# Two heads' value products in turns: a change to groups B and D of a two-layer hybrid decoder on Trainium2

## The chip, the cores and the metric

The kernel runs on one core of a Trainium2 chip, in one launch. The metric is the device time of an execution in microseconds (us), the median of several runs. Profiles are of one execution taken by the hardware profiler; times in them are counted from the first instruction.

Engines in the profile: PE is the matrix engine, PEld its weight loads, DVE is VectorE, ACT is ScalarE, POOL is GpSimd, SP issues most of the DMAs. Matrix products are written to PSUM, which has 8 banks. TensorE's two clock levels are 1.2 and 2.4 GHz; the profile shows the granted clock as a share of full speed.

## What is computed

One sequence of 1024 tokens with 1024 channels passes through two layers. Each layer has a token mixing part with four groups of 256 channels (4 heads of 64 each) and then a mixture of experts. The groups are: A (RWKV-7, a recurrence), B (stick-breaking attention), C (mLSTM, chunks) and D (attention over the 256 best keys of an indexer, one key and value head for all query heads). Cut to groups B and D:

```python
def stick_breaking_attn(q, k, v):                 # group B
    for i in range(S // 128):                     # blocks of 128 queries
        z = q[block i] . k[: 128 * (i + 1)] * scale
        ...
        outs.append(einsum('bhqk,bkhd->bqhd', att, v[:, :kl]))

def dsa_attn(q, k, v, qi, ki, wi):                # group D
    for i in range(S // 128):
        ...
        prob = softmax(logits of the chosen keys)
        outs.append(einsum('bhqn,bqnd->bhqd', prob, vs))   # one v for all heads
```

The value product of a block, a head and 128 keys is the piece of the last line of each: 64 value channels by 128 queries, summed over the key blocks 0 to i.

## The kernel before

A layer's mixing part is written as Python generators that a planner, weave (L196), takes in turns by a virtual time: each step of a stream adds the matrix work that it issued, or 0.2 where it issued none, both over the stream's pace. The program order that comes out is the order of priority; a scheduler then places each instruction in the queue of its engine when its inputs are expected, and each engine executes its queue in order. After the projections, four streams run side by side: group A (pace 260); group D, then C, then B (paces 350 and 140, one after the other in one stream); the modulation vectors (the ada weights); and the output projection, which waits for finished pieces of the groups.

Groups B and D run over two column tiles ct of two heads each, two groups f of four blocks, and the blocks i of 128 queries. For each block two generators, one per head, are stepped in turns. In B (Stick.unit, L561) a head's steps are: scores into PSUM tag "a", a copy to z, Exp and Ln into e; then a mask on POOL, a reversed running sum on DVE (L580), a subtraction (L582), Exp; then transposes of z on PE (L148), a copy of them into at, which is e's memory, and the value products. B has three pairs of z and e, handed round as (2i + h) mod 3. In D (Dsa.unit, L1112) a head has two steps, with z ("dz") and at ("dat") from a shared pool of 23 large tiles.

The products of a head stand at the end of its last step. The output tile py has 128 partitions: head 0 of the pair fills partitions 0 to 63 and head 1 partitions 64 to 127, which are the two halves of PE's columns. py comes from PSUM tag "b", which has three banks that group A and others share. It is taken by whichever head comes first, and copied out when both heads are done. All products go through the helper k.mm, so their line in the profile is L143; in the profile B's products are b<-e,sv and D's are b<-dat,dv. They are fp32, 128 rows by 64 columns with 128 elements of moving data, and the profile shows each as two records. In group A, b<-tl, pj<-tl,ra and pj<-ra,tl are an inverse by doubling, ya the output. Group C has one product of the same kind as the value products, b<-v,kw (L793), whose loop over heads alternates the halves.

Copies out of PSUM by k.ev go to DVE and ACT in turns, by one counter for all streams.

Of the kernel before, what the change touches and what calls it, by code (L numbers as in the profile page):

```python
# [244 lines left out]
class Rwkv:  # L245
# [261 lines left out]
    def run(self, width=3):  # L507
        self.job = {}
        jobs = [(ct, hf) for hf in range(2) for ct in range(2)]
        yield from self.prep(*jobs[0])  # L510
        units = [(ct, 0, nb) for ct in range(2) for nb in range(4)] + [(ct, 1, nb) for nb in range(4) for ct in range(2)]
        ahead = {(0, 0, 1): jobs[1], (1, 0, 0): jobs[2], (1, 0, 2): jobs[3]}
        live, side = [], []
        k = self.k
        free = [(k.med("ra"), k.med("bkv", 384), k.med("mp"), k.big("tl", 1024)) for _ in range(width)]
        while units or live or side:
            while units and len(live) < width and units[0][:2] in self.job and "bon" in self.job[units[0][:2]]:
                u = units.pop(0)
                own = free.pop(0)
                live.append((u, self.unit(*u, own), own))  # L520
                if u in ahead:
                    side.append(self.prep(*ahead[u]))
            for it in list(live):
                try:
                    next(it[1])
                    yield
                except StopIteration:
                    live.remove(it)
                    free.append(it[2])
                    if it[0][2] % 2:  # L530
                        side.append(self.out(*it[0][:2], it[0][2] // 2))
            for g in list(side):
                try:
                    next(g)
                    yield
                except StopIteration:
                    side.remove(g)
# [13 lines left out]
    V.scalar_tensor_tensor(y, y, g, sq, op0=ALU.mult, op1=ALU.mult)  # L551


class Stick:


# [1 line left out]
        self.k, self.pc = k, pc  # L558
        self.qk, self.y, self.done = {}, {}, set()

    def unit(self, i, h, py, own):  # L561
        k, nc = self.k, self.k.nc
        V, G = nc.vector, nc.gpsimd
        hs = slice(64 * (h % 2), 64 * (h % 2) + 64)
        q, kt = self.qk[i // 4, h // 2]
        q = q[:, 512 * (h % 2) + 128 * (i % 4):512 * (h % 2) + 128 * (i % 4) + 128]
        kl = 128 * (i + 1)
        z, e = own
        for o in range(0, kl, 512):
            n = min(512, kl - o)  # L570
            pz = k.psum("a", n)
            k.mm(pz, q, kt[h % 2][0][:, o:o + n], stop=False)
            k.mm(pz, q, kt[h % 2][1][:, o:o + n], start=False)
            V.tensor_scalar(z[:, o:o + n], pz, 40.0, None, op0=ALU.min)
        k.act(e[:, :kl], z[:, :kl], AF.Exp)
        k.act(e[:, :kl], e[:, :kl], AF.Ln, bias=1.0)
        yield
        dg = slice(kl - 128, kl)
        G.tensor_tensor(e[:, dg], e[:, dg], k.c("sl"), op=ALU.mult)
        V.tensor_tensor_scan(e[:, :kl][:, ::-1], e[:, :kl][:, ::-1], e[:, :kl][:, ::-1], initial=0.0,  # L580
                             op0=ALU.add, op1=ALU.bypass)
        V.tensor_tensor(z[:, :kl], z[:, :kl], e[:, :kl], op=ALU.subtract)  # L582
        k.act(z[:, :kl], z[:, :kl], AF.Exp)
        G.tensor_tensor(z[:, dg], z[:, dg], k.c("sl"), op=ALU.mult)
        yield
        at = e
        for o in range(0, kl, 512):
            n = min(512, kl - o)
            pt = k.psum("a", n)
            for b in range(n // 128):  # L590
                k.tr(pt[:, 128 * b:128 * b + 128], z[:, o + 128 * b:o + 128 * b + 128])
            k.ev(at[:, o:o + n], pt)
        if not py:
            py.append(k.psum("b", 128))
        for b in range(i + 1):
            k.mm(py[0][hs], self.v[:, b, hs], at[:, 128 * b:128 * b + 128],
                 start=b == 0, stop=b == i)
        yield

    def run(self, tk, l):  # L600
        k = self.k
        groups = [(f, ct) for f in range(2) for ct in range(2)]
        own = [(k.big("z"), k.big("e")) for _ in range(3)]
        self.load(tk, l, *groups[0])
        for g, (f, ct) in enumerate(groups):
            if g > 1:
                self.load(tk, l, f, ct)
            n = 4 * f + 4
            self.v = k.big("sv", 128 * n).rearrange("p (n c) -> p n c", n=n)
            k.nc.sync.dma_start(self.v, tk.pk[l][0:128 * n, 128 * ct:128 * ct + 128].rearrange("(n p) c -> p n c", p=P))  # L610
            y = k.med("yb")
            self.y[ct, f] = y
            for i in range(4 * f, 4 * f + 4):
                if i == 2 and g == 0:
                    self.load(tk, l, *groups[1])
                py = []
                gens = [self.unit(i, 2 * ct + h, py, own[(2 * i + h) % 3]) for h in range(2)]
                while gens:
                    for n in list(gens):
                        try:  # L620
                            next(n)
                            yield
                        except StopIteration:
                            gens.remove(n)
                k.ev(y[:, 128 * (i % 4):128 * (i % 4) + 128], py[0])
            head_norm(k, y, self.pc("sbg", ct), eps=self.eps)
            self.done.add((ct, f))
            yield
# [233 lines left out]
class Dsa:  # L862
# [246 lines left out]
            V.tensor_scalar(key[i], key[i], 1.0, -NEG, op0=ALU.subtract, op1=ALU.mult)  # L1109
            yield 4.0  # L1110

    def unit(self, i, h, py):  # L1112
        k, nc = self.k, self.k.nc
        V = nc.vector
        kl = 128 * (i + 1)
        hs = slice(64 * (h % 2), 64 * (h % 2) + 64)
        o = 512 * (h % 2) + 128 * (i % 4)
        q = self.q[i // 4, h // 2][:, o:o + 128]
        neg = self.neg[i] if i >= 2 else self.zd[:, 256 - kl:256]
        z = k.big("dz")  # L1120
        mx = k.small("dmx", 2, bufs=4)
        for o in range(0, kl, 512):
            n = min(512, kl - o)
            p = k.psum("a", n)
            k.mm(p, q, self.kh[:, o:o + n], stop=False)
            k.mm(p, q, self.kl[:, o:o + n], start=False)
            V.tensor_tensor_reduce(z[:, o:o + n], p, neg[:, o:o + n], 1.0, 2 * NEG if o == 0 else mx[:, 0:1],
                                   op0=ALU.add, op1=ALU.max, accum_out=mx[:, 0:1] if o == 0 else mx[:, 1:2])
        last = mx[:, 0:1] if kl <= 512 else mx[:, 1:2]
        nb = k.small("dnb", 1, bufs=4)  # L1130
        V.tensor_scalar(nb, last, -0.125, None, op0=ALU.mult)
        k.act(z[:, :kl], z[:, :kl], AF.Exp, scale=0.125, bias=nb, accum_out=self.ssum[:, 4 * i + h:4 * i + h + 1])
        yield
        at = k.big("dat")
        for o in range(0, kl, 512):
            n = min(512, kl - o)
            pt = k.psum("pj", n)
            for b in range(n // 128):
                k.tr(pt[:, 128 * b:128 * b + 128], z[:, o + 128 * b:o + 128 * b + 128])
            k.ev(at[:, o:o + n], pt)  # L1140
        if not py:
            py.append(k.psum("b", 128))
        for b in range(i + 1):
            k.mm(py[0][hs], self.v[:, b, :], at[:, 128 * b:128 * b + 128], start=b == 0, stop=b == i)
        yield

    def load(self, f, ct):
# [6 lines left out]
    def run(self):  # L1154
        k = self.k
        self.y, self.q = {}, {}
        groups = [(f, ct) for f in range(2) for ct in range(2)]
        self.load(*groups[0])
        for g, (f, ct) in enumerate(groups):
            y = k.med("yd")  # L1160
            self.y[ct, f] = y
            for i in range(4 * f, 4 * f + 4):
                if i % 4 == 2 and g < 3:
                    self.load(*groups[g + 1])
                py = []
                gens = [self.unit(i, 2 * ct + h, py) for h in range(2)]
                while gens:
                    for n in list(gens):
                        try:
                            next(n)  # L1170
                            yield
                        except StopIteration:
                            gens.remove(n)
                k.ev(y[:, 128 * (i % 4):128 * (i % 4) + 128], py[0])
            if ct:
                yield from self.finish(f)

# [1024 lines left out]
```

## Time and profile before

| | |
|---|---|
| median of 3 runs | 3668.0 us (3665.5 to 3668.82) |
| profiled execution, timed | 3678.16 us |
| its span in the profile | 3676.4 us |
| granted TensorE clock, mean | 0.922 |
| busy PE / DVE / ACT / POOL | 88% / 76% / 53% / 23% |
| mixing part of layer 0, groups D, C, B | 430 to 1215 us |
| mixing part of layer 1, groups D, C, B | 2280 to 3030 us |
| experts | 1215 to 1900 us and 3030 us to the end |

The page gives one line of busy time per engine, 40 slices, the DMA queues, the chain of work that ended last, and the costliest groups of instructions. A matrix instruction's start is recorded and its end is modelled, so records overlap and a busy PE is not PE at its peak. What one stretch is limited by is read from views that are cut to that stretch.

### The profile page before, as it was taken

How to read it: one execution, taken by the hardware profiler on the slowest of the kernel's cores; microseconds unless marked ns; L12 is line 12 of the kernel's file. 1: busy time of each engine (PE TensorE's matmuls, PEld its weight loads, DVE VectorE, ACT ScalarE, POOL GpSimd, SP SyncE). 2: the span in 40 equal slices, each digit the busy share in tenths (PEclk: the TensorE clock that was granted, in tenths of full speed). 3: DMA queues.
4: the chain of work that ended last, by engine and by line, in shares of the span. 5: the costliest groups of instructions: out<-in, count | busy, mean ns of one | idle time of the engine just before them, and what ended most of it. 6: DMA issues, size and time to landing. Idle time of an engine off the chain costs nothing.

```text
span 3676.4 us, 54588 instructions
## 1 busy us (share of the span) xinstructions
PE 3234.4 (88%) x18848; PEld 2542.0 (69%) x18848; DVE 2779.7 (76%) x5552; ACT 1935.2 (53%) x3324; POOL 841.2 (23%) x769
## 2 busy tenths in 40 slices
PE   6888889998888799999958888999898879999996
PEld 3876645576667678777757766767676667877775
DVE  4589843457766799999965998555777679999995
ACT  3456332234444577777753662432444447777774
POOL 3220110113322113322312202111223221342221
PEclk8989999998998899999979888989998879999998
DMA  5222355433433899999931233023344369999996
GB/s 195 76 87 91 118 189 195 168 125 98 135 115 140 277 363 385 379 385 383 357 116 53 92 93 102 17 70 111 112 128 118 118 241 364 381 380 387 383 381 216
DMA packets 373671, 746.61 MB, mean 203 GB/s; under 512 B 44235, under 2 KB 108385, under 8 KB 373393
## 3 DMA queue, kind: packets, MB, share of 16 engines
q1 hardware_dynamic: 346880, 672.03, 51.0%
q0 software_dynamic: 20256, 70.33, 7.3%
q8 instruction: 150, 2.46, 0.3%
q10 hardware_dynamic: 6256, 0.74, 0.1%
q14 instruction: 129, 1.05, 0.1%
HBM read 635.45 MB, written 107.53 MB: 202 GB/s over the span
## 4 chain that ended last, share of the span: by engine, by line
PE 49%; DVE 21%; DMA 18%; issue 5%; ACT 4%; POOL 1%; SPq 1%; ACTq 0%; DVEq 0%; POOLq 0%
PE pj L143 25%; PE b L143 16%; DMA wr<-in_moe_w_dram 12%; DVE dkey L1017 5%; PE a L143 3%; PE a L148 3%; DVE e L580 1%; PE pj L148 1%; DMA out_dram<-yo,si 1%; DVE wl L1530 1%; DMA xs<-yo,si 1%; PE b L148 1%; DVE z L582 1%; ACT wh L160 1%; DVE h L1780 1%
## 5 line engine op out<-in xcount | busy, mean ns | idle before, releaser
L160 ACT ACTIVATE wh<-wr 128x1024 fp32r<-128x1024 f32 (+3 forms) x900 | 888.6, 1005 | 296.6 <-DMA wr<-in_moe_w_dram 133.1
L1530 DVE TENSOR_TENSOR wl<-wr,wh 128x1024 fp32r<-128x1024 f32 x792 | 938.3, 1220 | 59.7 <-ACT wh L160 47.7
L143 PE MATMUL pj<-wl,xh 128*128 128x512 f32 x1056 | 419.3, 403 | 15.9 <-DVE wl L1530 15.4
L143 PE MATMUL pj<-wh,xh 128*128 128x512 f32 x1056 | 421.2, 400 | 11.3 <-ACT xh L160 11.2
L143 PE MATMUL pj<-wh,xl 128*128 128x512 f32 x1056 | 419.7, 397 | 0.0
L143 PEld LDWEIGHTS pj<-wl,xh 128*128 128x128 f32 x1056 | 200.0, 190 | 83.6 <-DVE wl L1530 39.4
L143 PEld LDWEIGHTS pj<-wh,xh 128*128 128x128 f32 x1056 | 200.1, 190 | 55.5 <-ACT xh L160 13.8
L143 PEld LDWEIGHTS pj<-wh,xl 128*128 128x128 f32 x1056 | 200.6, 190 | 45.8 <-DVE xl L1542 0.8
L143 PE MATMUL b<-wh,hh 128*128 128x512 f32 x528 | 210.5, 399 | 12.3 <-ACT wh L160 11.3
L1426 POOL DMA_INDIRECT xg<-h2d,si x64 | 74.7, 1167 | 630.9 <-PE a L148 375.7
L143 PE MATMUL pj<-hh,wh 128*128 128x512 f32 x480 | 197.4, 412 | 14.6 <-ACT wh L160 5.7
L143 PE MATMUL b<-wh,hl 128*128 128x512 f32 x528 | 208.2, 394 | 0.7 <-DVE hl L1542 0.7
L143 PE MATMUL pj<-hh,wl 128*128 128x512 f32 x480 | 196.3, 409 | 6.4 <-DVE wl L1855 6.4
L143 PE MATMUL pj<-wh,hh 128*128 128x256 f32 (+2 forms) x640 | 187.6, 306 | 16.1 <-DVE stl L1972 11.6
L143 PE MATMUL pj<-wh,hl 128*128 128x256 f32 (+2 forms) x640 | 192.4, 302 | 3.3 <-DVE hl L1832 3.3
L143 PE MATMUL pj<-hl,wh 128*128 128x512 f32 x480 | 194.4, 405 | 0.0
L143 PE MATMUL pj<-wl,hh 128*128 128x256 f32 (+2 forms) x640 | 188.9, 297 | 2.8 <-POOL wl L1855 2.8
L160 ACT ACTIVATE ra<-b 128x256 f32<-128x256 f32 x192 | 73.2, 383 | 222.5 <-PE b L143 220.2
L143 PE MATMUL b<-wl,hh 128*128 128x512 f32 x528 | 175.1, 410 | 2.2 <-DVE wl L1530 2.1
L1497 POOL DMA_INDIRECT out_dram<-yo,si x32 | 141.4, 4419 | 137.4 <-DVE yo L1494 122.7
L1497 POOL DMA_INDIRECT xs<-yo,si x32 | 136.3, 4260 | 133.5 <-DVE yo L1494 119.4
L421 DVE TENSOR_TENSOR tl<-pj,tl 128x512 f32<-128x512 f32 x128 | 87.1, 686 | 99.0 <-PE pj L143 98.0
(524 smaller groups left out, 7819.6 us busy)
## 6 DMA issues: line engine op xcount, KB each, us to landing
wr<-in_moe_w_dram SPq DMA_DIRECT2D x792, 512.0 KB
aw<-in_ada_w_dram SPq DMA_DIRECT2D x96, 512.0 KB
wr<-in_w_in_dram SPq DMA_DIRECT2D x84, 256.0 KB
wo<-in_w_out_dram SPq DMA_DIRECT2D x48, 256.0 KB
xs<-xp SPq DMA_DIRECT2D x48, 256.0 KB
xp<-xs SPq DMA_DIRECT2D x48, 256.0 KB
out_dram<-xp SPq DMA_DIRECT2D x48, 256.0 KB
sk<-pt SPq DMA_DIRECT2D x32, 256.0 KB
```

The source lines that it names most:

```text
L143: return self.nc.tensor.matmul(out, lhsT, rhs, start=start, stop=stop, skip_group_check=True)
L148: return self.nc.tensor.transpose(out, in_, self.c("ident")[o:o + n, o:o + n])
L160: i = self.nc.scalar.activation(out, in_, f, **kw)
L421: V.tensor_tensor(tt, pT, tt, op=ALU.add)
L580: V.tensor_tensor_scan(e[:, :kl][:, ::-1], e[:, :kl][:, ::-1], e[:, :kl][:, ::-1], initial=0.0, op0=ALU.add, op1=ALU.bypass)
L582: V.tensor_tensor(z[:, :kl], z[:, :kl], e[:, :kl], op=ALU.subtract)
L1017: V.tensor_scalar(junk[j % 3 - 1][:, :width(i)], keys[i], v, None, op0=ALU.is_ge, op1=ALU.add, accum_out=cnt[:, j:j + 1])
L1426: i = self.k.nc.gpsimd.indirect_dma_start(out=xg, out_offset=None, in_=self.h2d, in_offset=bass.IndirectOffsetOnAxis(ap=gi.bitcast(U32), a ...
L1497: k.nc.gpsimd.indirect_dma_start(out=self.xs, out_offset=bass.IndirectOffsetOnAxis(ap=si.bitcast(U32), axis=0), in_=yo, in_offset=None, co ...
L1530: i = nc.vector.tensor_tensor(wl, raw, wh.bitcast(F32), op=ALU.subtract)
L1780: V.scalar_tensor_tensor(hs[i], xs[i], ms[:, 2 + i:3 + i], s, op0=ALU.mult, op1=ALU.mult)
```

## The change

The two heads' generators no longer issue products. Each appends its tile at to a list, and when both are done a new function issues the products of both, key block by key block, first head 0 and then head 1, so that the halves of the columns alternate in program order. py is taken there. One yield stands between the products and the copy of py. Group B and group D get the same edit (in B the two heads have weights of their own, v[:, b, hs]; in D both load v[:, b, :]).

```diff
+def values(k, i, ats, v):
+
+    py = k.psum("b", 128)
+    for b in range(i + 1):
+        for h, at in enumerate(ats):
+            hs = slice(64 * h, 64 * h + 64)
+            k.mm(py[hs], v(b, hs), at[:, 128 * b:128 * b + 128], start=b == 0, stop=b == i)
+    return py
...
-    def unit(self, i, h, py, own):
+    def unit(self, i, h, ats, own):
...
             k.ev(at[:, o:o + n], pt)
-        if not py:
-            py.append(k.psum("b", 128))
-        for b in range(i + 1):
-            k.mm(py[0][hs], self.v[:, b, hs], at[:, 128 * b:128 * b + 128],
-                 start=b == 0, stop=b == i)
+        ats.append(at)
         yield
...
-                py = []
-                gens = [self.unit(i, 2 * ct + h, py, own[(2 * i + h) % 3]) for h in range(2)]
+                ats = []
+                gens = [self.unit(i, 2 * ct + h, ats, own[(2 * i + h) % 3]) for h in range(2)]
...
-                k.ev(y[:, 128 * (i % 4):128 * (i % 4) + 128], py[0])
+                py = values(k, i, ats, lambda b, hs: self.v[:, b, hs])
+                yield
+                k.ev(y[:, 128 * (i % 4):128 * (i % 4) + 128], py)
```

## Rows read from the trace of the kernel before

**Rows 1.** The page: span, and busy time of each engine with its share.

```profile
span 3676.4 us, 54588 instructions
PE 3234.4 (88%) x18848; PEld 2542.0 (69%) x18848; DVE 2779.7 (76%) x5552; ACT 1935.2 (53%) x3324; POOL 841.2 (23%) x769
```

**Rows 2.** Busy us by stretch: length, PE, PEld, DVE, ACT, POOL; clock, DMA.

```profile
430.00:680.00 250.00, 231.49 (x1463) 130.44 (x1462) 115.86 (x297) 82.53 (x201) 28.47 (x48) 0.95 0.55 186
...
845.00:1142.00 297.00, 257.30 (x2118) 206.46 (x2118) 207.57 (x382) 134.02 (x293) 83.11 (x111) 0.90 0.37 113
2280.00:2425.00 145.00, 134.46 (x1057) 102.92 (x1055) 87.11 (x253) 62.32 (x159) 20.48 (x33) 0.95 0.18 56
...
2600.00:2910.00 310.00, 262.81 (x2129) 211.25 (x2129) 215.19 (x385) 135.70 (x298) 90.69 (x115) 0.88 0.36 110
```

**Rows 3.** Chain of waits, shares by line: 430 to 680, 2280 to 2425, 845 to 1142.

```profile
by line: PE pj L143 34.2%; PE b L143 27.6%; PE pj L148 8.4%; PE a L143 7.9%; issue 6.0%; DMA aw<-in_ada_w_dram 5.3%; DVE ca L676 2.0%; POOL ca L674 1.0%; SPq L298 0.9%; ACT sq L160 0.8%; ACT dz L160 0.7%; DMA modd<-am 0.7%; PE b L148 0.6%; 
...
by line: PE b L143 41.5%; PE pj L143 16.1%; PE a L143 13.5%; PE pj L148 12.1%; DVE cs L315 1.6%; issue 1.6%; DVE dat L186 1.5%; ACT dz L160 1.5%; ACT sq L160 1.3%; ACT dat L160 1.3%; DVE dz L1127 1.1%; DVE cs L320 1.0%; DVE tl L421 0.9%; DV
...
by line: PE b L143 26.6%; PE pj L143 18.2%; DVE e L580 7.3%; PE a L148 5.9%; PE a L143 5.6%; issue 3.9%; DVE z L582 3.9%; DVE z L574 2.6%; DMA sk<-pt 2.4%; ACT z L160 2.4%; POOL z L584 2.1%; ACT e L160 1.4%; DMA mod<-modd 1.3%; POOL tl L392
```

**Rows 4.** Busy time by stretch, products alone (PE, PEld first): D's two, B's two.

```profile
430.00:680.00 250.00, 41.64 (x288) 30.74 (x288) 13.88 (x24) 11.26 (x24) 0.95 0.55 186
...
2280.00:2425.00 145.00, 40.51 (x288) 30.10 (x286) 13.57 (x23) 10.96 (x23) 0.95 0.18 56
...
845.00:1142.00 297.00, 38.85 (x288) 30.62 (x288) 0.90 0.37 113
...
2600.00:2910.00 310.00, 39.48 (x288) 31.15 (x288) 0.88 0.36 110
```

**Rows 5.** Timeline of PE: start, length, instruction, how many merged.

```profile
2375.72 1.96 PE L143 MATMUL b<-dat,dv 128*64 128x128 f32 x16
2377.61 0.45 PE L143 MATMUL b<-bkv,mp 64*64 64x64 f32 x8
...
1127.00 2.89 PE L143 MATMUL b<-e,sv 128*64 128x128 f32 x28
...
1040.12 1.09 PE L143 MATMUL b<-e,sv 128*64 128x128 f32 x8
1041.14 0.71 PE L143 MATMUL b<-tl 128*128 128x128 f32 x4
```

**Rows 6.** Timeline of PE at group C's alternating product.

```profile
711.36 0.45 PE L143 MATMUL b<-v,kw 128*64 128x65 f32 x8 [1.01 <-DVE kw L789]
```

**Rows 7.** By tile: length of one record in ns, least, median and most.

```profile
L143 PE MATMUL b<-v,kw x56: 220/222/368, 711.4 to 820.4; 128*64 128x65 f32 x56
...
L143 PEld LDWEIGHTS b<-e,sv x576: 132/137/232, 847.2 to 2906.5; 128*64 128x64 f32 x192
L143 PE MATMUL b<-e,sv x576: 272/273/477, 847.2 to 2906.6; 128*64 128x128 f32 x192
```

**Rows 8.** Timeline of PE in B's last block of layer 0.

```profile
1132.95 1.09 PE L143 MATMUL b<-e,sv 128*64 128x128 f32 x8 [0.25 <-ACT e L160]
...
1139.55 1.09 PE L143 MATMUL b<-e,sv 128*64 128x128 f32 x8 [0.43 <-ACT e L160]
```

**Rows 9.** Timeline of ACT and DVE around the end of groups A and B, layer 0.

```profile
1128.78 1.06 ACT L160 ACTIVATE e<-z 128x1024 f32<-128x1024 f32 x1 [0.88 <-PE b L143]
...
1130.11 0.28 DVE L186 COPY yb<-b 128x128 f32<-128x128 f32 x1
1130.31 0.41 DVE L503 TENSOR_TENSOR ya<-sqh,b 128x256 f32<-128x256 f32 x1
...
1142.28 0.28 ACT L160 ACTIVATE yb<-b 128x128 f32<-128x128 f32 x1 [0.42 <-PE b L143]
```

**Rows 10.** Timeline of weight loads: D's products, then group C's alternating product.

```profile
2375.72 1.72 PEld L143 LDWEIGHTS b<-dat,dv 128*64 128x64 f32 x16
...
711.36 0.31 PEld L143 LDWEIGHTS b<-v,kw 128*64 128x64 f32 x8 [1.24 <-DVE kw L789]
```

More of the change, by code (lines that the diff above doesn't have):

```diff
@@ L559, in __init__ @@
         self.qk, self.y, self.done = {}, {}, set()
-    def unit(self, i, h, py, own):
+    def unit(self, i, h, ats, own):
         k, nc = self.k, self.k.nc
         V, G = nc.vector, nc.gpsimd
-        hs = slice(64 * (h % 2), 64 * (h % 2) + 64)
         q, kt = self.qk[i // 4, h // 2]
@@ L1110, in search, with unit @@
             yield 4.0
-    def unit(self, i, h, py):
+    def unit(self, i, h, ats):
         k, nc = self.k, self.k.nc
@@ L1115, in unit @@
         kl = 128 * (i + 1)
-        hs = slice(64 * (h % 2), 64 * (h % 2) + 64)
         o = 512 * (h % 2) + 128 * (i % 4)
@@ L1140, in unit @@
             k.ev(at[:, o:o + n], pt)
[L1141 to L1144, printed above, removed]
+        ats.append(at)
         yield
@@ L1164, in run @@
                     self.load(*groups[g + 1])
-                py = []
-                gens = [self.unit(i, 2 * ct + h, py) for h in range(2)]
+                ats = []
+                gens = [self.unit(i, 2 * ct + h, ats) for h in range(2)]
                 while gens:
@@ L1173, in run @@
                             gens.remove(n)
-                k.ev(y[:, 128 * (i % 4):128 * (i % 4) + 128], py[0])
+                py = values(k, i, ats, lambda b, hs: self.v[:, b, :])
+                yield
+                k.ev(y[:, 128 * (i % 4):128 * (i % 4) + 128], py)
             if ct:
```

## Prediction

> **What bounds the kernel now.** I read the page first: the profiled execution spans 3676.4 us (3678.16 us as timed, 10 us or 0.3% above the median of 3668.0), and TensorE is the busiest engine at 88%, VectorE next at 76% [rows 1]. The change touches only the mixing stages of the two layers, so the second view is busy time by stretch [rows 2]. Group D runs at 430 to 680 us in layer 0 and 2280 to 2425 us in layer 1; PE is busy 231.49 of 250 us and 134.46 of 145 us there (93% in both), VectorE 46% and 60%. Group B runs at 845 to 1142 us and 2600 to 2910 us; PE is busy 257.30 of 297 us and 262.81 of 310 us (87% and 85%), VectorE 70% and 69%. So D's stretches are PE's own, B's are shared. The third view, the chain of waits cut to a stretch, says the same [rows 3]: in D of layer 1, PE lines alone hold over 83% (41.5 + 16.1 + 13.5 + 12.1); in B of layer 0 they hold 56% (26.6 + 18.2 + 5.9 + 5.6), and VectorE's scan L580 (7.3%) and L582, L574 and waits on ACT and POOL take part of the rest. The fourth view cuts the second to the products themselves [rows 4]: 288 records in each of the four stretches, busy 41.64, 40.51, 38.85 and 39.48 us, 160.5 us in all. A product is two records (per layer and group 144 products: 36 blocks times 4 heads).
>
> **What the change does to PE.** It removes no product and adds none; 1152 records stay. What is new is that the products of the two heads, which write different halves of the columns, stand in turns in PE's queue. Today 16 records of one half run 1.96 us [rows 5]. One record lasts 0.273 us from start to end [rows 7], so 15 steps take 1.69 us: 0.113 us a step, one after the other. The trace holds one place where products of the same kind (128 rows, 64 columns, fp32, one PSUM bank) already alternate between halves: the state update of group C, line 793. Its 8 records of 65 columns run 0.45 us [rows 6]. One lasts 0.222 us [rows 7]; a serial step would be 0.113 x 65/128 = 0.057 us, so 7 steps and one length would make 0.62 us, while 3 steps make 0.39 us. 0.45 us is three steps and a slow first one: two records in each step. A second sign lies in B: where the two heads happen to stand back to back, 28 records run 2.89 us [rows 5] where 27 steps and one length would be 3.32 us, so the second head began under the first. I conclude that a pair of heads will cost what one head costs today.
>
> **The first term.** By steps: block i has 4(i+1) records in 4(i+1) steps now and in 2(i+1) after. Over i = 0 to 7 that is 72 steps less, 72 x 0.113 = 8.1 us for each of 8 passes (two column tiles, two groups, two layers): 65 us. By busy time, half of 160.5 us is 80 us; this also halves what a run costs at its two ends (16 records from 2375.72 to the next instruction at 2377.61 take 1.89 us, 0.08 us more than 16 steps [rows 5]). Where the heads are back to back, some is already gained. I take **72 us of PE time, 36 in D and 36 in B**, with 65 and 80 as ends.
>
> **How much of it reaches the end.** PE executes in the order of its queue, so an instruction of group A behind the products is late by them: group A's inverse (b<-tl) begins at 1041.14 us, right behind 8 of B's products that began at 1040.12 [rows 5]. In D, PE is idle only 18.5 of 250 and 10.5 of 145 us [rows 2]; what is late next is, in layer 0, the DMA of the ada weights (5.3% of the chain, 13 us, [rows 3]), which PE will meet sooner. I let 0.8 through: 29 us (ends 0.6 and 1: 22 and 36). In B, PE's share of the chain is 56%; what is late next is VectorE's scan and the exponentials of the same heads, a serial sequence that a faster product shortens only at its end. There the latency hardly falls: after the last head's transposes 2(i+1) records follow today, and 2(i+1) steps follow then. I let 0.5 through: 18 us (ends 0 and 36). Sum 47 us.
>
> **What the change adds.** (a) The first head's products wait for the second head's transposes and copies. In layer 0's last block they begin at 1132.95 us and the second head's at 1139.55 [rows 8]; they filled PE while the second head's scan ran, and will no longer. The work behind them on PE is group A's and the output projection's, which moves up, so PE itself loses nothing; what can lose is the owner of the first head's buffer. B has three z/e pairs, and the second head of the next block takes the first head's. Today the exponential at 1128.78 waited 0.88 us for just those products [rows 9]; after it waits for 30 to 32 records in half the steps instead of 14 to 16 in all, some 0 to 1 us more, at the few blocks where it waits at all. D's tiles come from a shared pool of 23 and are held longer by the same few us. I take 1 us a layer. (b) One bank of three of tag b is now taken when the first head is done: in that block from 1132.95 to the copy at 1142.28, 9.4 us [rows 8, 9]; after, only from the second head on. Group A uses the same three. That can only free something; no row prices it, it lies within PE's idle time of rows 2, and I take nothing. (c) Each block gets one more yield, 0.2 in the weave's virtual time. A pair of heads counts some 5 on average, so B falls back by 4% of its 297 us, about 12 us of place against group A, and D likewise. That is work that changes places, not new work, but B is already last: group A's last sub-block is finished at 1130.31 us and B's last copy starts at 1142.28 [rows 9]. Price 0 to 12 us a layer; I take 3, since the queue lets B's ready work move up. Instruction counts of ACT, VectorE, POOL, SP and all DMAs stay the same; copies alternate between VectorE and ACT by a counter that other streams share, so some swap engines, priced at nothing since both are below 71% busy in these stretches. (a) to (c): 8 us.
>
> One rule of the Trainium skill speaks against the change. The rows first: 16 weight loads of one half take 1.72 us [rows 10] and 0.137 us each [rows 7], 2.19 us if end to end, so loads already run under products that use the same 128 rows; in group C 8 alternating loads take 0.31 us [rows 10]. The page "TensorE: Matmul & The Clock Gate" (Part 3: Packing small matmuls, The mechanism) says that a weight load overlaps a running product only where the row group differs, and both heads use all rows. By that rule a step would be a load and a product; the trace disagrees, and I give it 0.02 below.
>
> **How the numbers follow.** 47 - 8 = 39 us less: 3678 - 39 = 3639 us for the profiled execution, and from the median 3668 - 39 = **3629 us**. Band of this case 3612 to 3645 us (D 22 to 36, B 9 to 27, less 4 to 14). Chance 0.52.
>
> **Rivals.**
> - B is bound by its own sequence, not by PE: VectorE's 70% and PE's 40 idle us [rows 2] speak for it, the products on the chain against it. B gives 0, D 29, added 12: 3651 us. Chance 0.18.
> - All of it comes through: PE's time bounds group A as well, the bank freed in (b) helps. 72 to 80 less 4: about 3596 us. Chance 0.13. For it speaks D's 93%; against it the VectorE part of B's chain.
> - **Slower**: B, last already, loses so much place that whole blocks of it run alone after group A is done. A block alone takes from 1130.11 to 1142.28 us, 12.2 us [rows 9]. It decides from two more blocks alone in each layer (4 x 12.2 = 49 us against a gain of 47); at three it is 6 x 12.2 - 47 = +26 us less what of the gain is lost with it, about 3699 us. Against it: 12 us of place is one block, not three. Chance 0.08.
> - Two records do not share a step here, only the additions remain: 3668 to 3676 us. Rows 6 speak against. Chance 0.03.
> - The halves take turns but each load stands open ahead of its product: 0.137 + 0.113 = 0.250 us for two records instead of 0.226, 576 x 0.024 = 14 us more on PE, 9 of it through, and 8 added: 3685 us. Chance 0.02.
> - The queues' order falls differently with no sign that I can argue: 0.04, mostly within the bound.
>
> The measurement of this kernel can tell about 0.2% (7 us) from no change. Faster: 0.52 + 0.18 + 0.13 = 0.83. Slower: 0.08 + 0.02 + 0.01 = 0.11. Same: 0.06. For 8 in 10 the range runs from the rival of full gain to just below the bound: 3594 to 3664 us.
>
> **What would show it.** Products' busy time per stretch of about 20 us instead of 39 to 42, with 32 records in about 2 us; D's stretches shorter by 12 to 16 us each and B's by 5 to 14. If products halve and B's stretch keeps its length, the B rival is right; if the distance from group A's last product to B's last copy grows from 12 us to 35 or more, the slower rival is. If 32 records still take 3.5 us, the first term is wrong. The expert stages (1215 to 1900 us, 3030 us on) should keep their length.

## The result, and the profile after

The changed kernel takes 3613.8 us (median of 4 runs, 3610.4 to 3617.2), 53 us less than the kernel before in the same comparison (3666.8 us): a ratio of 0.985 (0.9836 to 0.9864). The profiled execution took 3611.5 us, its span is 3609.7 us and its mean granted clock 0.922, as before. It lies 2 us below its median, and that of before 11 us above the 3666.8, so the two profiles differ by 66.7 us where the medians differ by 53.

The page of the changed kernel, lines as in [rows 1]:

```profile
span 3609.7 us, 54562 instructions
PE 3185.2 (88%) x18836; PEld 2491.4 (69%) x18848; DVE 2778.3 (77%) x5552; ACT 1928.5 (53%) x3324; POOL 900.9 (25%) x769
```

PE is busy 49 us less; VectorE and ScalarE did the same work. Busy time by stretch (columns as in [rows 2]): D, C, B of layer 0, then of layer 1, each cut from D's first product to its last copy, to B's first product, to B's last copy:

```profile
455.00:652.00 197.00, 183.41 (x1325) 97.95 (x1322) 93.31 (x261) 65.76 (x164) 21.70 (x35) 0.96 0.60 204
652.00:830.00 178.00, 159.33 (x1191) 120.16 (x1193) 107.43 (x248) 57.06 (x158) 32.45 (x44) 0.92 0.43 142
830.00:1118.00 288.00, 250.57 (x2065) 196.14 (x2065) 206.18 (x372) 130.66 (x284) 90.05 (x110) 0.89 0.36 111
2252.00:2381.00 129.00, 117.47 (x1063) 90.10 (x1064) 86.40 (x258) 65.03 (x165) 20.45 (x31) 0.93 0.21 63
2381.00:2554.00 173.00, 151.85 (x1139) 120.53 (x1144) 106.17 (x247) 56.48 (x157) 35.06 (x44) 0.90 0.28 91
2554.00:2845.00 291.00, 253.97 (x2066) 198.31 (x2067) 209.22 (x372) 130.78 (x285) 87.47 (x110) 0.87 0.36 110
```

The kernel before, cut in the same way:

```profile
457.00:664.00 207.00, 196.43 (x1313) 110.49 (x1311) 91.83 (x257) 63.17 (x158) 21.33 (x36) 0.96 0.55 184
664.00:847.00 183.00, 161.57 (x1156) 118.73 (x1154) 105.18 (x244) 57.95 (x156) 31.70 (x42) 0.91 0.44 147
847.00:1142.00 295.00, 256.83 (x2117) 206.28 (x2117) 205.86 (x378) 132.49 (x290) 82.63 (x110) 0.90 0.37 114
...
2279.00:2425.00 146.00, 135.46 (x1058) 103.21 (x1057) 87.42 (x253) 62.32 (x159) 20.48 (x33) 0.95 0.19 58
2425.00:2605.00 180.00, 157.93 (x1097) 123.90 (x1097) 103.60 (x242) 57.49 (x155) 31.77 (x41) 0.85 0.26 85
2605.00:2907.00 302.00, 260.54 (x2119) 209.99 (x2120) 209.99 (x379) 132.61 (x292) 85.10 (x110) 0.89 0.37 111
```

The rows are cut at whole microseconds; by the marks themselves the kernel before has 208, 183, 295 and 145, 181, 301 us. So D lost 10 and 16 us, C 4 and 7, B 8 and 11: 56 of the 66.7. The rest is spread over the other stages; the longest of them, which holds layer 0's experts, kept its length (1059 us before, 1057 after). D is still PE's own (183 of 197, 117 of 129 us busy), B still shared. So say the chains of waits of layer 1's D and layer 0's B, shares by line, as in [rows 3]:

```profile
by line: PE b L143 32.6%; PE pj L143 15.5%; PE a L143 14.4%; PE pj L148 14.3%; ACT sq L160 2.9%; ACT dz L160 2.5%; issue 2.5%; DVE cs L315 2.1%; DVE dz L1133 1.6%; DVE dat L186 1.5%; DVE ks L314 1.2%; DVE ar L338 1.2%; DVE kn L311 1.1%; DVE
...
by line: PE pj L143 21.5%; PE b L143 20.8%; DVE e L589 7.9%; PE a L143 5.6%; PE a L148 5.3%; issue 4.8%; DVE z L591 3.9%; ACT e L160 3.2%; DMA sk<-pt 2.4%; ACT z L160 2.3%; DVE z L583 1.9%; DVE e L186 1.8%; DMA xp<-xs 1.7%; DVE xp L2121 1.7
```

PE lines hold 77% in D (before 83%) and 53% in B (before 56%); in B the scan (now L589) comes next, as before.

The products alone, stretches that hold all of D's, then B's, of each layer [rows 4]:

```profile
430.00:668.00 238.00, 25.73 (x288) 17.61 (x288) 13.89 (x24) 11.32 (x24) 0.95 0.59 205
2240.00:2390.00 150.00, 25.77 (x288) 18.29 (x288) 13.88 (x24) 11.26 (x24) 0.92 0.21 65
...
815.00:1125.00 310.00, 30.03 (x288) 21.07 (x288) 0.89 0.38 117
2545.00:2850.00 305.00, 30.62 (x288) 21.43 (x288) 0.87 0.38 116
```

288 records in each, as before, but busy 26 and 30 us, not 39 to 42. PE's timeline, columns as in [rows 5], at D's last pair of heads in layer 0 and at B's last:

```profile
650.16 1.97 PE L143 MATMUL b<-dat,dv 128*64 128x128 f32 x32
652.06 0.44 PE L148 MATMUL b<-cst,tl 128*128 128x128 f32 x2
...
1112.24 0.69 PE L143 MATMUL b<-e,sv 128*64 128x128 f32 x2
1112.86 1.11 PE L148 MATMUL a<-cst,z 128*128 128x128 f32 x4
1113.90 1.98 PE L143 MATMUL b<-e,sv 128*64 128x128 f32 x16
```

32 records of two heads run 1.97 us, where 16 of one head ran 1.96 [rows 5]. The second place shows what the diff does not: two records, the first head's first product, stand alone at 1112.24 us, ahead of the second head's last transposes, with the rest behind these. That product needs nothing of the second head, so the scheduler places it earlier. D's 576 records come in 61 unbroken runs and B's in 62, where whole pairs would be 32 each.

### The profile page after: what moved, and what is told of

Same layout as the page of the kernel before. It is cut to its first block, busy times and chain, and to the rows that moved or that the text cites. A ratio compares the mean times of both kernels' runs of the same rounds, so it can differ in the third digit from the quotient of the medians.

```text
span 3609.7 us, 54562 instructions
## 1 busy us (share of the span) xinstructions
PE 3185.2 (88%) x18836; PEld 2491.4 (69%) x18848; DVE 2778.3 (77%) x5552; ACT 1928.5 (53%) x3324; POOL 900.9 (25%) x769
## 4 chain that ended last, share of the span: by engine, by line
PE 47%; DVE 21%; DMA 18%; issue 7%; ACT 4%; POOL 2%; SPq 1%; ACTq 0%; DVEq 0%; POOLq 0%
PE pj L143 26%; PE b L143 14%; DMA wr<-in_moe_w_dram 11%; DVE dkey L1024 4%; PE a L143 3%; PE a L148 2%; DMA xs<-yo,si 2%; DVE wl L1535 2%; DVE e L589 1%; PE pj L148 1%; ACT wh L160 1%; PE b L148 1%; DVE h L1785 1%; DVE yo L1499 1%; DVE z L591 1%
## 5 line engine op out<-in xcount | busy, mean ns | idle before, releaser
L143 PE MATMUL pj<-wh,xh 128*128 128x512 f32 x1056 | 421.5, 400 | 11.2 <-ACT xh L160 9.2
L1502 POOL DMA_INDIRECT xs<-yo,si x32 | 164.1, 5127 | 134.0 <-DVE yo L1499 117.6
L1502 POOL DMA_INDIRECT out_dram<-yo,si x32 | 160.9, 5027 | 134.1 <-DVE yo L1499 117.5
```

What stands on the lines that cost most here:

```text
L143: return self.nc.tensor.matmul(out, lhsT, rhs, start=start, stop=stop, skip_group_check=True)
L1502: k.nc.gpsimd.indirect_dma_start(out=self.xs, out_offset=bass.IndirectOffsetOnAxis(ap=si.bitcast(U32), axis=0), in_=yo, in_offset=None, co ...
```

## The experiments

Each kernel was timed beside runs of the kernel before on the same chip (medians 3667.1 to 3667.9 us); ratios are to those. All but the parts alone edit both groups, and all compute the full result.

One measure is used throughout. The granted clock has two levels, full (2.4 GHz) and half (1.2 GHz). From a stretch's length I take half of its half-clock time, by the clock records of the trace: its length *at full clock*. Length times granted clock is the same but for rounding: B of layer 0 before is 295 x 0.90 = 266 us, 266.3 by the records. The measure is a way of counting: it treats all time at half clock as if PE set the pace in it, and so takes off too much where PE waits.

**The turns undone.** The block's products stay together at the new place, head by head.

```diff
-    for b in range(i + 1):
-        for h, at in enumerate(ats):
+    for h, at in enumerate(ats):
+        for b in range(i + 1):
```

> The changed kernel with the two loops of the new function swapped: both heads' products still come after both heads are done, with the added yield, but head 0's all stand before head 1's. Only the turns are undone. If the gain of 53 us is the shared steps on PE, it is gone: 3660 to 3676 us, and the products' busy time is back to about 39 to 41 us a stretch. If half or more of it comes from the later place of the products and the planner's other order, 3640 us or less remains.

Measured: 3656.4 us, ratio 0.9973 (0.9959 to 0.9988), 4 us below the range that I had given for no gain at all. The turns are worth 42.6 us here; the rest of the edit (one place for both heads, the yield, the order that follows) took 10.7 us off, where I had put 8 us on. In this kernel's view of the products alone, D's two and B's two:

```profile
430.00:680.00 250.00, 39.04 (x288) 29.22 (x288) 13.89 (x24) 11.31 (x24) 0.95 0.53 185
2280.00:2435.00 155.00, 37.24 (x288) 29.28 (x288) 13.87 (x24) 11.22 (x24) 0.91 0.20 63
...
850.00:1155.00 305.00, 41.38 (x288) 32.85 (x288) 0.89 0.36 111
2600.00:2900.00 300.00, 41.24 (x288) 32.96 (x288) 0.91 0.37 115
```

158.9 us of busy time against 112.2 with the turns: 47 us, close to the 42.6 of the time. D's last pair of layer 0 in its timeline:

```profile
670.50 3.33 PE L143 MATMUL b<-dat,dv 128*64 128x128 f32 x32
```

3.33 us against 1.97, with the same neighbours on both sides.

**The added yield taken out.**

```diff
                 py = values(k, i, ats, lambda b, hs: self.v[:, b, hs])
-                yield
                 k.ev(y[:, 128 * (i % 4):128 * (i % 4) + 128], py)
```

> The changed kernel without the added yield. The yield alone cost 21 us on the kernel before. If that holds here, 3593 us. If the cost there came from the order that fell out and not from the yield, 3614 within 10, with span times mean clock near 3328.

Measured: 3647.4 us, ratio 0.9951 (0.9932 to 0.997): without the yield 34 us slower than with it, and in neither of my two cases. **The yield alone, added to the kernel before**, gives the opposite sign.

```diff
                         except StopIteration:
                             gens.remove(n)
+                yield
                 k.ev(y[:, 128 * (i % 4):128 * (i % 4) + 128], py[0])
```

> The kernel before with one more yield ahead of the copy of py in both groups, and nothing else: the planner's place alone. The prediction priced it at 3 us a layer, 3671 to 3676 us. If the 16 us that PE's saved time (37 us by start to next start) doesn't explain come from the planner's other order, 3650 to 3658 us.

Measured: 3688.8 us, ratio 1.006 (1.0037 to 1.0083), 22 us slower with it. So a yield has no fixed price: it gives another order, and the order has one. B's stretch of layer 0 without the yield, and the longest waits of PE in it (total us, times, longest):

```profile
829.00:1128.00 299.00, 241.98 (x2109) 190.60 (x2110) 208.25 (x377) 130.97 (x290) 85.66 (x110) 0.91 0.36 112
...
PE a L148 <- ACT z L160: 18.4, 8, 11.2
PE pj L143 <- ACT ra L160: 4.5, 6, 1.6
```

The waits in the changed kernel's stretch:

```profile
PE a L148 <- ACT z L160: 10.1, 9, 2.8
PE b L143 <- DVE e L186: 4.5, 5, 2.2
```

The transposes wait 18.4 us for the exponential in z, not 10.1, and 11.2 of the 18.4 fall in one place; PE stood idle meanwhile. In all it is idle 57 us of this stretch (299 less 242), against 37 in the changed kernel (288 less 251). This is a part of the 34 us; the rest was not followed.

**The second head first,** so that the product that stands first belongs to the head that is ready last, and none can go ahead.

```diff
-        for h, at in enumerate(ats):
+        for h, at in reversed(list(enumerate(ats))):
```

> The changed kernel with the second head first in each turn. In the changed kernel the first head's first product is ready early and is queued by itself (61 and 62 runs of products on PE instead of 32 and 32); with the second head first nothing is ready before both are, so runs stay whole and the bank is taken later. If a run's ends cost some 0.2 us each, 58 runs less give 8 to 12 us at full clock: 3602 to 3606 us, and span times mean clock falls from 3328 to about 3318. If the lone product cost nothing (it fills a gap): 3614 us. If the bank taken early was what let the copies go in time: slower.

Measured: 3618.8 us, ratio 0.9856 (0.9838 to 0.9874). The products' busy time falls to the 20 us a stretch of the prediction in D, and to 24 and 26 in B:

```profile
430.00:680.00 250.00, 20.17 (x288) 15.42 (x288) 13.89 (x24) 11.30 (x24) 0.95 0.57 201
2260.00:2400.00 140.00, 20.39 (x288) 15.44 (x288) 13.86 (x24) 11.31 (x24) 0.93 0.21 66
...
835.00:1130.00 295.00, 25.58 (x288) 20.06 (x288) 0.88 0.36 112
2560.00:2850.00 290.00, 24.36 (x288) 19.03 (x288) 0.88 0.37 113
```

90.5 us, 21.7 less than in the changed kernel, and no time gained by it, where I had put 8 to 12 us. No run of two records is left, and the runs are 39 in D and 38 in B. So the lone first products cost PE busy time and no time that shows. Whether they lie in gaps of PE's, or this order loses elsewhere what it saves here, is not shown: the four orders by head below differ by up to 29 us among themselves.

**Half the charge to the planner,** since a pair costs PE what one head did.

```diff
             k.mm(py[hs], v(b, hs), at[:, 128 * b:128 * b + 128], start=b == 0, stop=b == i)
+    k.pe -= (i + 1) * 128 / 600
     return py
```

> The changed kernel with the planner told that a turn of two products costs what one did (its virtual matrix time halved in the new function); nothing else differs but the order of the streams. In the changed kernel group A ends 31 to 33 us before B in each layer, before it was 12. If that tail costs, A and B end closer together and the time falls by 5 to 20 us: 3594 to 3609. If place is worth nothing: 3614 within 6, with span times clock unchanged at 3328 and only the half-clock time different.

Measured: 3629.2 us, ratio 0.989 (0.9871 to 0.9908), 15 us slower than the changed kernel, outside both of my cases. D and B come earlier against group A: B's last copy of layer 0 and group A's last product on ScalarE and VectorE [rows 9] now stand the other way round:

```profile
1123.32 0.28 ACT L160 ACTIVATE yb<-b 128x128 f32<-128x128 f32 x1 [5.39 <-PE b L143]
...
1140.21 0.42 DVE L503 TENSOR_TENSOR ya<-sqh,b 128x256 f32<-128x256 f32 x1
```

In the changed kernel they stand so, B 31 us after A:

```profile
1086.84 0.42 DVE L503 TENSOR_TENSOR ya<-sqh,b 128x256 f32<-128x256 f32 x1
...
1118.13 0.28 ACT L160 ACTIVATE yb<-b 128x128 f32<-128x128 f32 x1 [0.57 <-PE b L143]
```

The kernel in which A comes last is the slower one here, so B's ending long after A need not be a loss.

**The turns undone in three more orders.** The three orders so far differ from the changed kernel's by 5 to 34 us, up to four fifths of the 42.6 us, so these might have been an order's luck. The three kernels above were run with the loops swapped as in the first experiment; planner charges, yields and the order of the streams stay as they were.

> The changed kernel without the added yield, and with the products of a block head by head: it differs from the run without the yield (3647.4 us) in the turns alone, as the run with the products head by head (3656.4 us) differs from the changed kernel (3613.8 us). Theory, the turns have a price of their own: the distance is 43 us here as it was there, so 3690 us (3678 to 3702), and the stretches of D and B times their granted clock are longer by 10 to 18 us and 7 to 14 us. Rival, the 43 us were in good part a lucky order of the queues: the distance falls anywhere between 0 and 80 us, and the stretches times the clock don't say the same as the time.

> The changed kernel with half the matrix work charged to the planner for the products (3629.2 us with the turns), and the products of a block head by head; the order in which the streams are taken is that of the run at half the charge, so the two differ in the turns alone. Theory: 3629 + 43 = 3672 us (3660 to 3684). Rival, order: any distance between 0 and 80 us.

> The changed kernel with the second head's products first (3618.8 us with the turns), and all of the second head's products before the first head's. It differs from the run with the second head first in the turns alone. Theory: 3619 + 43 = 3662 us (3650 to 3674). Rival, order: any distance between 0 and 80 us. If the three distances of this call lie within 10 us of 43, the turns' price holds in four orders; if they scatter by more than 20 us, the mean of the four is the price and the scatter is the order's.

Measured: 3680.7 us, ratio 1.0028 (1.0016 to 1.0041); 3668.7 us, 1.0002 (0.999 to 1.0015); 3651.9 us, 0.9958 (0.994 to 0.9976). All in us; "busy" is the fall of the products' busy time, D and B the fall of their stretches (both layers) at full clock:

| order | turns | by head | time | busy, D + B | D | B |
|---|---|---|---|---|---|---|
| as changed | 3613.8 | 3656.4 | 42.6 | 24.8 + 22.0 | 29.6 | 20.7 |
| no yield | 3647.4 | 3680.7 | 33.3 | 22.7 + 26.0 | 18.6 | 13.1 |
| half the charge | 3629.2 | 3668.7 | 39.4 | 25.7 + 26.8 | 27.4 | 12.1 |
| second head first | 3618.8 | 3651.9 | 33.1 | 21.1 + 22.3 | 19.7 | 12.4 |
| mean | | | 37.1 | 23.6 + 24.3 | 23.8 | 14.6 |

The distances lie within 10 us of 43: the turns have a price of their own, 37 us on the mean. The rest of the edit has none: without turns the four orders stand 11 us below the kernel before, 13 above, 1 above and 16 below. Taken as span times mean clock over each kernel's runs, the turns are worth 50, 38, 34 and 38 us in the four orders. The kernels by head are not quite without shared steps: where one head's records follow the other's, 10 to 24 pairs of records in each group start together, and 55 with the second head first, of 288 possible; with turns it is 228 to 288.

The busy time in the table is at the clock as granted. Counted at full clock as well, by the clock records, it falls by 23.2 us in D and 20.7 in B on the mean. So in D all of PE's saved time comes through (23.8 of 23.2, between 0.8 and 1.2 of it in the single orders), in B 0.7 of it (14.6 of 20.7, between 0.55 and 1.0).

**One group alone.** The edit in D alone, and in B alone (the latter on two chips).

> The edit in group D alone. The prediction gave D 29 of 47 us; scaled to the 53 us measured, 3634 us. If the stretches of the changed kernel's trace are read at their face (D 26, C 12, B 19 us shorter) and C's gain belongs to D, 3629; if C's gain comes from B, 3641.

> The edit in group B alone. The prediction gave B 18 of 47 us less its share of the additions: scaled, 3648 us. If B is bound by its own sequence: 3662 or more. If the two edits help each other, the two single gains sum to clearly less than 53 us; if they are independent, to 53 within 8.

> The edit in group B alone once more, for a profile at the usual clock. In the profiles so far span times mean granted clock, the time that PE would need at full clock, is 3390 us before, 3328 changed, 3355 with D alone, 3385 head by head and 3393 with the yield alone. If the pairs' gains in that measure add up, B alone gives 3390 - 62 + 35 = about 3363, with its time near 3664 again through more half-clock time than before. If B alone truly gains nothing: 3385 to 3395.

Measured: D alone 3669.2 us, ratio 1.0 (0.9983 to 1.0017); B alone 3664.1 us, 0.9994 (0.9979 to 1.0008), and 3660.8 us, 0.9976 (0.9958 to 0.9994). Nothing or next to it from either, 53 us from both; for D alone I had expected 26 to 38 us. At full clock the parts do not differ so from the whole. Span times mean clock, averaged over each kernel's runs, is 3395 us before, 3362 with D alone, 3370 and 3374 with B alone (3377 in its profile, between my two cases) and 3331 with both: 33, 21 to 25 and 64 us less. What is left of the span, the cost of the half clock by this measure, rises against the kernel before by 35, 12 to 22 and 10 us. So by this count each part saves its share, and what takes it back in the parts is time at half clock. To see where D's gain goes, **D alone was run with its products head by head**:

> The edit in group D alone, with the products of a block head by head: beside the run with the edit in D alone (3669.2 us with the turns) it differs in D's turns alone, in the same order of the streams. In the four orders with the edit in both groups, turns shortened D's two stretches by 8 to 18 us and -1 to 14 us, some 22 us in all on the mean. Theory, D's turns are worth 22 us here too, and the edit in D alone came out at no change because moving the products behind the second head, with the added yield, cost as much in that order: 3691 us (3681 to 3701). Rival, what D gains is given back in B as long as B is unchanged: 3669 us (3660 to 3676).

Measured: 3678.2 us, ratio 1.0034 (1.002 to 1.0047), 9 us above D alone with the turns: between theory (22) and rival (0). The profiles say why. D alone with turns, D and B of layer 0, then of layer 1:

```profile
457.00:655.00 198.00, 184.50 (x1326) 98.51 (x1327) 93.61 (x262) 65.83 (x165) 21.69 (x35) 0.95 0.59 204
834.00:1150.00 316.00, 276.00 (x2101) 219.14 (x2101) 212.65 (x374) 132.66 (x287) 91.35 (x110) 0.84 0.34 105
2282.00:2411.00 129.00, 117.44 (x1060) 90.26 (x1059) 86.00 (x258) 65.00 (x165) 20.39 (x31) 0.93 0.19 62
2586.00:2897.00 311.00, 270.58 (x2101) 213.28 (x2101) 213.53 (x374) 131.60 (x287) 88.14 (x110) 0.87 0.34 106
```

and D alone, head by head:

```profile
459.00:674.00 215.00, 197.63 (x1323) 110.13 (x1322) 93.92 (x263) 65.55 (x164) 22.09 (x35) 0.96 0.55 190
848.00:1155.00 307.00, 267.55 (x2099) 211.33 (x2100) 211.57 (x376) 131.29 (x288) 90.62 (x110) 0.87 0.36 108
2288.00:2430.00 142.00, 130.78 (x1065) 102.26 (x1066) 89.27 (x260) 65.65 (x166) 20.08 (x31) 0.93 0.18 57
2602.00:2901.00 299.00, 264.81 (x2101) 210.18 (x2100) 213.29 (x374) 132.01 (x287) 89.17 (x110) 0.88 0.35 110
```

With the turns D is 17 and 13 us shorter, and B, which has none in either kernel, is 9 and 12 us longer. B does no more work: 2101 PE instructions in each layer against 2099 and 2101, and length times clock is 316 x 0.84 = 265 us against 307 x 0.87 = 267 in layer 0, 311 x 0.87 = 271 against 299 x 0.88 = 263 in layer 1. In layer 0 PE is idle for as long in both (40.0 and 39.5 us), and the 9 us are busy time of the same instructions at the lower clock; in layer 1 half of the 12 us is busy time and half is waiting. PE spends 60 us more at half clock in the whole execution (623.0 against 562.5 us), 39 of them in B and 19 in C. By the measure that costs 30 us, as much as D's turns give at full clock (17.3 + 12.5). In the medians 9 of the 30 us are left. With the turns, the longest spell that begins in B of layer 0 begins at 1072.5 us. Busy time just before it and in it, then PE's timeline at its start:

```profile
1068.00:1072.50 4.50, 2.32 (x14) 1.71 (x13) 4.43 (x12) 3.60 (x8) 2.42 (x4) 1.00 0.33 117
1072.50:1099.80 27.30, 19.61 (x89) 15.06 (x89) 15.08 (x25) 6.80 (x12) 7.85 (x7) 0.50 0.28 96
```

```profile
1069.99 0.33 PE L143 MATMUL b<-st,gt 64*64 64x64 f32 x4
1072.75 0.48 PE L143 MATMUL b<-rp,st 64*64 64x64 f32 x4 [2.43 <-DVE st L477]
```

PE stood idle 2.43 us for group A's state, the clock fell, and it stayed at half for 27 us in which PE was busy 19.6. That such a spell falls here in the one kernel and not in the other may come from where the gaps of group A and B happen to lie; that was not isolated. So the theory holds for D's work, and the rival for most of what came of it: what D gained was for the most part given back in C and B as time at half clock. B alone has no partner with its products head by head, and how much of its 3 to 7 us is the turns' stays open.

## Why the prediction was right, and where it was wrong

The forecast was 3629 us (3594 to 3664) with 0.83 for faster; 3613.8 is faster and in the range, 15 us below the forecast and 2 us inside the lower edge of the likeliest case's band (3612). The mechanism, shared steps on PE, was right. That the sum came so near is in part luck: three of its terms were off, and two of the errors cancelled.

**A pair of heads costs what one head costs: right.** 1.97 us for 32 records against 1.96 for 16 [rows 5], and 3.33 for the same 32 head by head. The sign read off group C's eight records [rows 6] held, and the rival without shared steps fell.

**Loads open: fell.** Where D's last pair runs, the timeline of weight loads shows

```profile
650.16 1.73 PEld L143 LDWEIGHTS b<-dat,dv 128*64 128x64 f32 x32 [0.17 <-issue]
```

32 loads in 1.73 us, where 16 took 1.72 [rows 10]: both halves are loaded within the steps of one. The Trainium skill's page "TensorE: Matmul & The Clock Gate" (Part 3: Packing small matmuls, The mechanism) lets a load overlap only where the row group differs. Here both heads use all 128 rows, and the measurement decides against it.

**The first term, 72 us of PE time: mis-sized.** It measured 47 us against the products head by head (43 to 52 over the four orders), 49 on the page. The step that failed is "4(i+1) steps now and 2(i+1) after": it took for granted that both heads' records stand next to each other. D's records hold 24 runs of two records and B's 26, for 32 pairs of heads each: in most blocks the first head's first product goes alone. The rest still goes in turns, but the product that lost its partner is left alone at the end, so such a block has two steps more than I counted, and more runs. Of 288 possible pairs of records in each group, 238 start together in D and 242 in B. I had set about 20 us a stretch; 26 came in D and 30 in B (25 and 24 at full clock). With the second head first the products' busy time is 68 us below that of the products head by head in the changed kernel's order, near the 72. But that kernel is no faster, so the size of the term alone does not give the time.

**How much reaches the end: too low in D.** I let 0.8 through in D and 0.5 in B; the four orders give 1.0 and 0.7 at full clock. The views read for it [rows 2, 3] pointed the right way: the 93% busy stretch passes all on, the shared one part. A term too large times a share too small made 47, and that the changed kernel's own order gave 42.6 is luck to that extent; the mean of four is 37.

**The additions, 8 us: wrong in sign, and wrong in kind.** In the changed kernel's order they measure -10.7 us, over the four orders -16 to +13. I priced a wait of ScalarE's, a bank and a place in the planner's order; what the edit did was to reshuffle the queues of the whole mixing part, and I could read no sign for that from the trace of before. It makes up the 15 us by which the time is below the forecast: 18.7 from here, less 4.4 from the turns, and 1 from a kernel before that ran at 3667.1 beside the first experiment, not at 3668.0. The 10.7 us are this order's luck.

**(b), the bank: half wrong.** I had it taken "only from the second head on". The lone first product takes it at 1112.24 us, before the second head is through, and it is copied out at 1118.13: 5.9 us, not 9.4 [rows 8, 9], but still across the second head's transposes.

**B bound by its own sequence: fell.** By it B's stretch would keep its length; in all four orders its two stretches together are 12 to 21 us shorter at full clock with the turns. Part of it is true: 0.3 of what PE saved in B does not show in B's length.

**The slower rival: its sign came, its price did not.** From group A's last product to B's last copy the distance in layer 0 grew from 12 us [rows 9] to 31, short of the 35 that I had set, and the time fell. (Its 3699 us also go 5 us beyond its own sum, 3668 + 26.) I had taken B's end for blocks that run alone. But where A ends after B, at half the charge, the kernel is 15 us slower, so the distance is no measure of a loss.

**All of the gain through (3596 us): fell,** because the 72 us were 47 and in B only a part of them came through.

**Order without a sign, 0.04:** too little. Another order alone moved this kernel by -16 to +13 us in the four kernels by head, and by +22 with the yield alone; the range should have had that as a term.

## What to carry to other kernels

Fp32 products of two heads that each fill half of the columns run in the time of one when their records alternate in the queue; look for a place in the old trace where this already happens, and for whether the scheduler can pull one of them out of the pattern. Where a planner and a scheduler set the order, price the edit by comparing kernels that differ in the edit alone and share the order (here 33 to 43 us in four orders), since a new order alone moved the time by -16 to +13 us. When a shorter stage brings nothing, compare length times granted clock over the kernels' runs and then stage by stage, before looking for a new wait.

## What the runs showed of the hardware that I had not expected

The clock can take back a gain far from where it was made. Against the kernel before, D alone is 33 us shorter at full clock on the mean of its runs, its cost of the half clock is 35 us higher, and its time is the same. Between D alone with turns and by head, 60 us more at half clock stand against 30 us that D gained. B of layer 0, with its products untouched or head by head, has nearly the same length at full clock in four kernels (266.3 us before, 264.3 in the changed kernel's order by head, 265.4 and 269.0 with D alone), while its true length ran from 295 to 316 us with 58 to 102 us at half clock. In the three other orders by head it is 257 to 276 us, so the measure compares only kernels of like order. The longest spell that began in that B, 27 us at half in D alone, began behind 2.43 us in which PE waited. What decides where such spells fall stays open.
